# Row softmax with a relative-position bias: the bias table issued first, three one-row chunks at the head of the stream, one bias strip buffer in place of two

## The chip, the cores and the metric

The kernel runs on one core of one Trainium2 chip. The metric is the device time in microseconds (us) of the whole program. The engines are named as in the profile: DVE is VectorE, ACT is ScalarE, POOL is GpSimd, SP is the sync engine that only issues transfers here. TensorE is not used.

## The reference, cut to what matters

```python
B, H, S, max_rel = 2, 8, 2112, 16
rel = pos[:, None] - pos[None, :]
bias = rel_bias[:, np.clip(rel, -16, 16) + 16]       # (H, S, S), from a table of (H, 33)
x = logits + bias[None]
out = softmax(x, axis=-1)                             # float32, (B, H, S, S)
```

The logits are 285 MB and so is the result. There are about three passes of arithmetic over each element, so the kernel is a stream: load, add, exponential, multiply, store.

## The kernel before: the parts that the change and the argument touch

The 2112 rows of one head are cut in 64 blocks of 33 rows. Two heads (one "head pair" k) fill the 128 partitions, and a chunk is r rows of every block: normally r = 3, which is 3.24 MB and 25 KB per partition. One bias strip F for a head pair, 128 x 2144, serves all chunks of that pair, read at a shifted offset.

```python
fpool = ctx.enter_context(tc.tile_pool(name="fpool", bufs=2))    # bias strips
io = ctx.enter_context(tc.tile_pool(name="io", bufs=7))          # chunks of up to 3 rows
# ... (chunks: r = 3 everywhere, the very last three rows one by one)

NPRE = 2
pre = [load(c, nc.sync) for c in chunks[:NPRE]]                  # SP queue
rbB = const.tile([P, H // 2, 2, W], FP32, tag="rbB")
nc.scalar.dma_start(out=rbB, in_=...)                            # bias table, ACT's queue
# ... (masks; bias_rows(k) builds F with two passes of 128x2112 and small ones)

for n, c in enumerate(chunks):
    k, row, j, r = c
    if k != fk:
        F, fk = bias_rows(k), k
    L = pre[n] if n < NPRE else load(c, nc.gpsimd)               # POOL's queue
    nc.vector.tensor_tensor(out=L3, in0=L3, in1=F3, op=ALU.add)
    for i in range(r):
        nc.scalar.activation(out=x, in_=x, func=EXP, accum_out=tot[:, i : i + 1])
    nc.vector.reciprocal(out=tot[:, 0:r], in_=tot[:, 0:r])
    for i in range(r):
        nc.vector.tensor_scalar_mul(out=x, in0=x, scalar1=tot[:, i : i + 1])   # "normalisation"
    nc.sync.dma_start(out=rows(out, row, j, r), in_=L[:, 0 : r * S])           # SP queue
```

A scheduler decides the order of instructions on each engine, and puts in the waits. A buffer of `io` is loaded again ("reload") only when its store has landed.

The softmax here doesn't subtract the row's maximum and nothing guards it: scores larger than these inputs give would overflow.

## Time and profile before

| | before |
|---|---|
| time, median (range) | 1334.06 us (1333.89 to 1334.34, 6 runs) |
| span of the profile | 1332.3 us |
| bytes moved | 571.19 MB |
| rate from 120 to 1260 us | 433 GB/s |

First the page of the kernel before: the span, the engines' busy time, then for 40 equal slices of the span the busy share of the DMA engines in tenths and the rate.

```profile
span 1332.3 us, 1666 instructions
...
DVE 947.2 (71%) x473; ACT 524.9 (39%) x529; POOL 49.0 (4%) x94
...
DMA  9999999999999999999999999999999999999998
GB/s 392 415 402 432 432 435 431 434 431 434 431 434 430 434 431 433 432 432 434 432 434 430 434 432 433 432 434 431 433 434 432 432 432 434 431 432 432 433 428 372
```

DMA is busy in every slice, while DVE has 29% of the span to spare. The bytes at 432.5 GB/s (the steady rate, between 432 and 433) need 571.19 MB / 0.4325 MB per us = 1320.7 us. Only the difference, 11.6 us of the span, can be won by ordering at this rate. I use this "loss" throughout: the length of a stretch minus the bytes it moved divided by 0.4325.

The same kernel cut in windows. Columns: the window, its length, busy us (and number of instructions) of DVE, ACT and POOL, clock, DMA share, GB/s. A packet counts in the window where it starts, so the DMA share can exceed 1.

```profile
core 0: us, DVE busy (x) ACT busy (x) POOL busy (x), PEclk, DMA share, GB/s
0.00:12.00 12.00, 0.00 (x0) 0.00 (x0) 3.31 (x11) 1.00 0.86 319
12.00:54.00 42.00, 36.02 (x21) 19.79 (x20) 0.00 (x0) 1.00 1.01 433
54.00:58.00 4.00, 4.00 (x4) 4.00 (x5) 0.00 (x0) 1.00 0.71 304
58.00:66.00 8.00, 8.00 (x6) 1.28 (x2) 0.00 (x0) 1.00 0.96 409
66.00:69.00 3.00, 3.00 (x3) 1.50 (x1) 0.53 (x1) 1.00 0.96 406
69.00:77.00 8.00, 8.00 (x7) 4.45 (x6) 0.00 (x0) 1.00 1.05 348
...
120.00:1260.00 1140.00, 812.33 (x395) 452.00 (x456) 41.49 (x76) 1.00 1.00 433
```

Before 120 us the loss sits mainly in the first 12 us, at 54 to 58 us and at 66 to 77 us (another 4.8 us are lost after 120 us). The loads and stores that make it, from the timeline of the kernel before (start, duration, engine, line, operation, output<-input, count; a queue such as SPq is where a transfer is issued, and a count over 1 means that the duration covers several with gaps):

```profile
0.73 0.40 ACTq L71 DMA_DIRECT2D rbB<-in_rel_bias_dram  x1
0.74 0.86 SPq L64 DMA_DIRECT2D L<-in_logits_dram  x2
...
24.15 2.35 DVE L120 TENSOR_TENSOR F<-eq,rbP 128x2112 f32<-128x2112 f32 x1
26.42 20.08 DVE L140 TENSOR_TENSOR L<-L,F 128x6336 f32<-128x6336 f32 x3
...
53.22 7.46 DVE L148 TENSOR_SCALAR L<-L,tot 128x2112 f32<-128x2112 f32 x6
...
57.02 4.03 SPq L149 DMA_DIRECT2D out_dram<-L  x2
...
66.54 0.53 POOL L64 DMA_DIRECT2D L<-in_logits_dram  x1 [62.40 <-DMA out_dram<-L]
```

All seven buffers are filled by 56 us. The first store is issued at 57.02, the first reload at 66.54, when that store has landed. The first packet of that reload appears only at 72.48, 5.9 us after its issue. Note the line at 24.15: the second strip's first pass, which DVE runs ahead of the first add.

### The profile page before, as it was taken

The numbers are of one execution on the slowest core, as the hardware profiler recorded it, in microseconds if no ns is written. First come the engines' busy times: TensorE is split into PE (matmuls) and PEld (weight loads), VectorE is DVE, ScalarE is ACT, GpSimd is POOL, SyncE is SP. The second block draws the span as 40 slices with busy tenths as digits, with TensorE's granted clock in tenths as the row PEclk, the third lists the DMA queues.
The fourth block names the chain that finished last, engine by engine and source line by source line (L and its number), as shares of the span: only waits on it lengthen the run. The fifth ranks groups of instructions, "written<-read, shape, count | busy, mean of one in ns | idle before, by whom it ended". The sixth has DMA issues, their size and how long they took to land.

```text
span 1332.3 us, 1666 instructions
## 1 busy us (share of the span) xinstructions
DVE 947.2 (71%) x473; ACT 524.9 (39%) x529; POOL 49.0 (4%) x94
## 2 busy tenths in 40 slices
DVE  4997677669676677767966677766796677766773
ACT  0754334433344333443344333443334333443341
POOL 0000000000000000000000000000000000000000
DMA  9999999999999999999999999999999999999998
GB/s 392 415 402 432 432 435 431 434 431 434 431 434 430 434 431 433 432 432 434 432 434 430 434 432 433 432 434 431 433 434 432 432 432 434 431 432 432 433 428 372
DMA packets 26076, 571.19 MB, mean 429 GB/s; under 512 B 2896, under 2 KB 3024, under 8 KB 3024
## 3 DMA queue, kind: packets, MB, share of 16 engines
q1 hardware_dynamic: 13248, 291.97, 51.0%
q0 software_dynamic: 12672, 278.99, 48.8%
q10 hardware_dynamic: 144, 0.14, 0.0%
q14 instruction: 12, 0.10, 0.0%
HBM read 285.61 MB, written 285.47 MB: 429 GB/s over the span
## 4 chain that ended last, share of the span: by engine, by line
DMA 79%; DVE 11%; issue 7%; another core or an unknown queue 1%; ACT 0%; POOLq 0%; POOL 0%; ACTq 0%
DMA out_dram<-L 47%; DMA L<-in_logits_dram 30%; DVE L L148 6%; DVE L L140 4%; DMA rbB<-in_rel_bias_dram 1%; DVE F L121 0%; DVE F L120 0%; ACT L L144 0%; DVE tot L145 0%; POOLq L64 0%; POOL L L64 0%; DVE rest L100 0%; DVE rest L101 0%; DVE rbP L92 0%
## 5 line engine op out<-in xcount | busy, mean ns | idle before, releaser
L140 DVE TENSOR_TENSOR L<-L,F 128x6336 f32<-128x6336 f32 (+1 forms) x90 | 594.7, 6609 | 346.8 <-DMA L<-in_logits_dram 346.6
L144 ACT ACTIVATE L<-L 128x2112 f32<-128x2112 f32 x264 | 515.2, 1952 | 768.7 <-DVE L L140 756.5
L148 DVE TENSOR_SCALAR L<-L,tot 128x2112 f32<-128x2112 f32 x264 | 331.8, 1313 | 0.0
L64 POOL DMA_DIRECT2D L<-in_logits_dram x88 | 48.5, 551 | 1241.2 <-DMA out_dram<-L 1231.6
L144 ACT ACTIVATION_READ_ACCUMULATOR L<-L 128x1 f32 x264 | 49.2, 186 | 0.0
L145 DVE RECIPROCAL tot<-tot 128x3 f32<-128x3 f32 (+1 forms) x90 | 14.8, 167 | 0.9 <-ACT L L144 0.9
L91 DVE COPY rbP<-rbB 64x132 f32<-64x132 f32 x1 | 0.2, 223 | 17.9 <-DMA rbB<-in_rel_bias_dram 17.9
L121 DVE TENSOR_TENSOR F<-F,rest 128x2112 f32<-128x2112 f32 x4 | 9.4, 2344 | 0.0
L120 DVE TENSOR_TENSOR F<-eq,rbP 128x2112 f32<-128x2112 f32 x4 | 9.4, 2344 | 0.0
L144 ACT ACT_TABLE_LOAD x1 | 1.3, 1283 | 17.8 <-DMA L<-in_logits_dram 17.8
L101 DVE SCALAR_TENSOR_TENSOR rest<-gt,rbP,rest 128x64 f32<-128x64 f32 x4 | 1.0, 265 | 0.0
L100 DVE TENSOR_SCALAR rest<-lt,rbP 128x64 f32<-128x64 f32 x4 | 0.9, 240 | 0.0
L122 DVE COPY F<-rbP 128x16 f32<-128x16 f32 x4 | 0.7, 163 | 0.0
L123 DVE COPY F<-rbP 128x16 f32<-128x16 f32 x4 | 0.7, 167 | 0.0
L78 POOL IOTA qm<- 64x64 f32 x2 | 0.4, 176 | 0.4 <-PEq L175 0.4
L92 DVE COPY rbP<-rbB 64x132 f32<-64x132 f32 x1 | 0.2, 225 | 0.0
L89 DVE TENSOR_SCALAR lt<-qm 128x64 f32<-128x64 f32 x1 | 0.2, 186 | 0.0
L89 DVE TENSOR_SCALAR gt<-qm 128x64 f32<-128x64 f32 x1 | 0.2, 186 | 0.0
L89 DVE TENSOR_SCALAR eq<-qm 128x64 f32<-128x64 f32 x1 | 0.2, 185 | 0.0
L164 POOL MEMSET const-float32-0.0<- 128x1 f32 x1 | 0.1, 98 | 0.2 <-issue 0.2
L164 POOL MEMSET const-bfloat16-1.0<- 128x1 bf16 x1 | 0.1, 101 | 0.0
L164 POOL MEMSET const-float32-1.0<- 128x1 f32 x1 | 0.1, 98 | 0.0
(1 smaller groups left out, 0.1 us busy)
## 6 DMA issues: line engine op xcount, KB each, us to landing
out_dram<-L SPq DMA_DIRECT2D x87, 3168.0 KB, 38.2
L<-in_logits_dram POOLq DMA_DIRECT2D x85, 3168.0 KB, 25.7
L<-in_logits_dram SPq DMA_DIRECT2D x2, 3168.0 KB, 24.3
L<-in_logits_dram POOLq DMA_DIRECT2D x3, 1056.0 KB, 17.0
out_dram<-L SPq DMA_DIRECT2D x3, 1056.0 KB, 18.3
rbB<-in_rel_bias_dram ACTq DMA_DIRECT2D x1, 132.0 KB, 17.2
```

Source lines behind the costliest of these rows:

```text
L64: eng.dma_start(out=L[:, 0 : r * S], in_=rows(logits, row, j, r))
L89: nc.vector.tensor_scalar(out=m, in0=qm, scalar1=0.0, scalar2=None, op0=op)
L100: nc.vector.tensor_scalar(out=rest, in0=lt, scalar1=low, scalar2=None, op0=ALU.mult)
L101: nc.vector.scalar_tensor_tensor(out=rest, in0=gt, scalar=high, in1=rest, op0=ALU.mult, op1=ALU.add)
L120: nc.vector.tensor_tensor(out=blocks, in0=wide(eq), in1=rev, op=ALU.mult)
L121: nc.vector.tensor_tensor(out=blocks, in0=blocks, in1=wide(rest), op=ALU.add)
L122: nc.vector.tensor_copy(out=F[:, 0:MR], in_=low.to_broadcast([P, MR]))
L123: nc.vector.tensor_copy(out=F[:, FW - MR : FW], in_=high.to_broadcast([P, MR]))
L140: nc.vector.tensor_tensor(out=L3, in0=L3, in1=F3, op=ALU.add)
L144: nc.scalar.activation(out=x, in_=x, func=EXP, accum_out=tot[:, i : i + 1])
L145: nc.vector.reciprocal(out=tot[:, 0:r], in_=tot[:, 0:r])
L148: nc.vector.tensor_scalar_mul(out=x, in0=x, scalar1=tot[:, i : i + 1])
```

## The change

The intent is to have the pipeline start earlier: the table arrives first, the first three chunks are a third as long so that compute and stores begin sooner, and one strip buffer keeps the second strip's work from standing ahead of the first add.

```diff
--- before.py
+++ after.py
@@ -34,16 +34,17 @@
     FW = S + W - 1
 
     const = ctx.enter_context(tc.tile_pool(name="const", bufs=1))
-    fpool = ctx.enter_context(tc.tile_pool(name="fpool", bufs=2))
+    fpool = ctx.enter_context(tc.tile_pool(name="fpool", bufs=1))
     io = ctx.enter_context(tc.tile_pool(name="io", bufs=7))
     small = ctx.enter_context(tc.tile_pool(name="small", bufs=8))
 
     chunks = []
     for k in range(H // 2):
         for b in range(B):
-            last = k == H // 2 - 1 and b == B - 1
             sizes = [R] * (W // R)
-            if last:
+            if not chunks:
+                sizes = [1] * R + sizes[1:]
+            if k == H // 2 - 1 and b == B - 1:
                 sizes = sizes[:-1] + [1] * R
             j = 0
             for r in sizes:
@@ -64,14 +65,14 @@
         eng.dma_start(out=L[:, 0 : r * S], in_=rows(logits, row, j, r))
         return L
 
-    NPRE = 2
-    pre = [load(c, nc.sync) for c in chunks[:NPRE]]
-
     rbB = const.tile([P, H // 2, 2, W], FP32, tag="rbB")
     nc.scalar.dma_start(
         out=rbB,
         in_=bass.AP(tensor=rel_bias.tensor, offset=rel_bias.offset, ap=[[0, P], [1, H * W]]),
     )
+    NPRE = 4
+    pre = [load(c, nc.sync) for c in chunks[:NPRE]]
+
 
     qm = const.tile([P, NB], FP32, tag="qm")
     for p0 in (0, NB):
```

The number of chunks goes from 90 to 92. The prefill (what is loaded before any buffer is stored) goes from 7 x 3.24 = 22.7 MB to 3 x 1.08 + 4 x 3.24 = 16.2 MB, because a one-row chunk still takes a whole buffer.

## The prediction

> **What bounds it now.** DMA. The page gives 571.19 MB over a 1332.3 us span; its slices show DMA at nine tenths or more in 38 of 40, VectorE (DVE) 71% busy, ScalarE 39%. The transfer view cut into windows gives 433 GB/s from 92 to 1260 us, so at that rate the bytes alone need about 1320 us. The Trainium skill, "DMA: Bandwidth & Descriptors", section "Where 436 GB/s comes from", has a ceiling of 435 GB/s; the trace agrees within 1%. Only some 12 us are lost: about 6.7 (2.9 MB missing) before 92 us, about 5 after 1310 us.
>
> **The loss at the start (transfer view, windows).** 2 to 12 us runs at 329 to 359 GB/s; 54 to 58 us at 304, because all loads end at 56 and the first store leaves at 57.0; 72 to 77 us at 314, because the first reload is issued only at 66.5, when the first store has landed, and its packets appear at 72.2. The two holes miss 1.1 MB, 2.5 us.
>
> **What the change does.**
> 1. The bias table moves ahead in the program, but it was already first on ScalarE's queue (issued 0.73 us, loads 0.74). The order buys nothing. It took 17.2 us because its small packets alternate with 25 KB packets of two load queues (skill, same page, "Queues, rings and completion order": round robin between queues at packet granularity; the trace agrees: table and first load land together near 17.8). Beside 8.4 KB packets I estimate 6 to 9 us.
> 2. The second strip's first multiply (2.35 us) no longer sits ahead of the first add: strip ready 6.3 us after the table, first add at about 14 us instead of 26.4.
> 3. Three one-row chunks: first store issued at about 27 us, not 57. But VectorE's order puts two normalisations after the third add, the third after the fourth chunk's add. The stores also queue behind the fourth chunk's 3.2 MB load, so they move at about 38 us. The prefill falls from 22.7 to 16.2 MB, loads end near 41 us, and the first reload can be issued only near 42 and moves near 47: one hole of about 2 us near 45 in place of the two.
> 4. One strip buffer: at the three head changes the strip (two operations of 2.35 us) is built between the last add of one head pair and the first of the next. VectorE idles 4.5 us per 15 us chunk, stores take 38 us from issue to landing, and before already delayed that add by 5 us with transfers at 432. I expect nothing.
>
> On the critical path is only what refills DMA holes: estimate 1 to 4 us. Compute starting 12 us earlier is not 12 us saved.
>
> **Prediction.** 1332.3 us, range 1328.5 to 1335.5. Faster by over 2%: 0.01; within 2%: 0.98; slower by over 2%: 0.01.
>
> **What would show it.** Right: bytes unchanged; 432 to 433 GB/s in mid-run, head changes included (near 315, 645, 975 us); first add at 11 to 17 us; first store issued before 32 us; table landing in 6 to 10 us; the holes at 56 and 73 gone, one near 45; mean over the first 92 us up from 401 to 405-415 GB/s; tail unchanged. Step 4 is wrong if a head change drops below 425 GB/s; step 3 if more or larger holes appear.
>
> **What would make it wrong.** A longer stall of the reloads behind three small stores; a steady-state split between load and store queues in which a head change starves both; small packets less efficient than estimated; the tail shifting since chunk numbering moves by two.

## The result, and the profile after

| | before | after |
|---|---|---|
| time, median (range) | 1334.06 us (1333.89 to 1334.34, 6 runs) | 1339.94 us (1336.88 to 1340.91, 6 runs) |
| span of the profile | 1332.3 us | 1334.4 us (an execution of 1336.92 us) |
| loss of the profiled span until 120 us | 6.8 us | 8.8 us |
| loss of the profiled span after 120 us | 4.8 us | 4.9 us |

Ratios are the mean time of one kernel's fast runs over that of the other's of the same rounds, so not quite the ratio of the medians that are quoted. Here it is 1.0038, interval 1.0025 to 1.0051. The kernel became 0.4% slower, not 0.1% faster, and its times scatter over 4 us where those of before lie within half a us. The profile is of one of its faster executions.

The page of the kernel after, span, DMA busy tenths and rate:

```profile
span 1334.4 us, 1678 instructions
...
DMA  9999999999999999999999999999999999999998
GB/s 388 394 406 431 432 434 432 433 432 432 433 432 433 433 432 432 430 434 432 432 435 429 435 433 431 435 428 436 431 432 433 430 435 432 432 434 430 435 428 375
```

The second slice (33 to 67 us) is lower than before (394 for 415), the third a little higher (406 for 402), and from the fourth on the two differ by a few GB/s either way. The windows of the kernel after, with the columns of the table before:

```profile
0.00:12.00 12.00, 3.50 (x10) 1.28 (x1) 2.28 (x9) 1.00 0.87 309
12.00:54.00 42.00, 24.23 (x17) 10.77 (x11) 1.06 (x2) 1.00 1.00 418
54.00:58.00 4.00, 4.00 (x3) 2.05 (x3) 0.00 (x0) 1.00 0.90 374
58.00:66.00 8.00, 8.00 (x3) 7.22 (x9) 0.00 (x0) 1.00 0.97 417
66.00:69.00 3.00, 3.00 (x4) 3.00 (x4) 0.53 (x1) 1.00 0.63 135
69.00:77.00 8.00, 8.00 (x4) 3.51 (x5) 0.00 (x0) 1.00 1.01 393
...
120.00:1260.00 1140.00, 814.64 (x394) 451.93 (x457) 40.09 (x76) 1.00 1.00 432
```

The holes of before at 54 to 58 us and at 69 to 77 us have shrunk: 374 for 304 GB/s and 393 for 348. In their place is a deeper one at 66 to 69 us, 135 GB/s, and the stretch from 12 to 54 us runs at 418 instead of 433. In loss: 0 to 54 us 3.1 us before and 4.8 after; 54 to 78 us 3.5 and 3.6; 78 to 120 us 0.2 and 0.3. So between 54 and 78 us nothing was won, and the extra loss of this execution, 2.0 us, lies nearly all before 54 us. From 120 us on nothing differs in these two profiles. (This is one of the faster executions; the one under "again" lost more on both sides of 120 us.)

The timeline of the kernel after, the lines that answer to those of before:

```profile
14.79 2.36 DVE L141 TENSOR_TENSOR L<-L,F 128x2112 f32<-128x2112 f32 x1
...
32.33 1.83 SPq L150 DMA_DIRECT2D out_dram<-L  x2
...
42.61 6.76 DVE L141 TENSOR_TENSOR L<-L,F 128x6336 f32<-128x6336 f32 x1 [8.75 <-DMA L<-in_logits_dram]
...
49.29 1.31 DVE L149 TENSOR_SCALAR L<-L,tot 128x2112 f32<-128x2112 f32 x1
...
50.63 0.33 SPq L150 DMA_DIRECT2D out_dram<-L  x1
...
66.13 0.53 POOL L65 DMA_DIRECT2D L<-in_logits_dram  x1 [17.39 <-DMA out_dram<-L]
...
67.75 0.33 SPq L150 DMA_DIRECT2D out_dram<-L  x1
```

The compute does start 12 us earlier (first add at 14.79 for 26.42), and the first stores leave at 32.33 for 57.02. But the third small store leaves only at 50.63, because its normalisation (49.29) stands behind the add of the fourth chunk (42.61), which waits for that chunk's load. The last packets of this store are seen between 65 and 66 us, and only then is the buffer's reload issued, 66.13. The next store follows at 67.75. At that moment all earlier loads are through, and the queues are dry.

Part of why a 1.08 MB store takes 15 us shows in the transfer view of the kernel after from 57 to 63 us (queue, packets, MB, share of 16 engines; q0 is POOL's queue, here loads with 25 KB packets, q1 is SP's, here that store with 8.4 KB packets):

```profile
DMA packets 154, 2.49 MB, mean 415 GB/s; under 512 B 3, under 2 KB 3, under 8 KB 3
...
q0 software_dynamic: 75, 1.82, 70.5%
q1 hardware_dynamic: 79, 0.67, 26.3%
```

The two queues send about as many packets, 75 and 79, so the store gets 0.67 of 2.49 MB. The first of its packets appear at 54 us, 3.4 us after the issue; why so late is not shown.

### The profile page after: what moved, and what is told of

Read it like the earlier page. It is cut to its first block, busy times and chain, and to the rows that moved or that the text cites. A ratio compares the mean times of both kernels' runs of the same rounds, so it can differ in the third digit from the quotient of the medians.

```text
span 1334.4 us, 1678 instructions
## 1 busy us (share of the span) xinstructions
DVE 947.8 (71%) x477; ACT 525.1 (39%) x529; POOL 48.2 (4%) x94
## 4 chain that ended last, share of the span: by engine, by line
DMA 79%; DVE 10%; issue 8%; another core or an unknown queue 1%; ACT 0%; SPq 0%; POOLq 0%; POOL 0%; ACTq 0%
DMA out_dram<-L 44%; DMA L<-in_logits_dram 35%; DVE L L149 6%; DVE L L141 3%; DVE F L121 0%; ACT L L145 0%; SPq L65 0%; DVE tot L146 0%; POOLq L65 0%; POOL L L65 0%; ACTq L176 0%; ACTq L145 0%; POOLq L176 0%
```

## The experiments

All but the last three were timed in 5 rounds against the kernel before on the same chip. Theory A: the loss is in when the early stores land, above all the third small one, and so when their buffers can be reloaded. Rivals: the single strip stalls the head changes (B); the lead chunks shift the tail (C); small first packets beside the table lose the time in the first 6 us (D).

| run | median us (range) | ratio to before (interval) | loss to 120 us | loss after |
|---|---|---|---|---|
| again (the change, once more) | 1339.66 (1338.69 to 1341.29) | 1.0041 (1.0028 to 1.0053) | 10.5 | 7.6 |
| no_leads | 1330.71 (1330.65 to 1331.11) | 0.9974 (0.9960 to 0.9988) | 3.4 | 4.8 |
| two_strips | 1352.31 (1352.12 to 1352.54, 4 runs) | 1.0135 (1.0121 to 1.0149) | 19.4 | 10.1 |
| fourth_on_pool | 1332.39 (1332.24 to 1332.98) | 0.9986 (0.9974 to 0.9999) | 4.4 | 5.1 |
| one_strip | 1331.09 (1330.72 to 1331.15) | 0.9976 (0.9964 to 0.9989) | 3.5 | 5.0 |
| third_on_act | 1332.97 (1332.76 to 1333.16) | 0.9991 (0.9978 to 1.0003) | 4.9 | 5.2 |
| lead_in_one | 1331.17 (1331.01 to 1331.40) | 0.9977 (0.9964 to 0.9991) | 3.6 | 4.6 |
| slow_mul | 1339.84 (1339.54 to 1340.14) | 1.0042 (1.0030 to 1.0055) | 10.9 | 6.1 |
| table_on_sync | 1331.45 (1330.93 to 1331.53) | 0.9979 (0.9965 to 0.9992) | 4.1 | 4.8 |

The two losses are those of the profiled execution. The kernel before had medians of 1334.2 to 1334.4 us in these jobs.

### again: the change, unchanged

No edit.

> The changed kernel unchanged, to get more executions and a second profile. Its six timed runs fell in two groups, 1336.9 (two) and 1339.7 to 1340.9 (four), and the profile is of the lower one. Theory A (the reload of a buffer waits for small stores that crawl beside large load packets, and the queues run dry near 67 us): the two groups again, and if the profile falls in the upper group, the extra 3 us lie before 100 us as a longer or further hole in the transfers, with 432 to 433 GB/s after it. Rival B (one strip buffer stalls the three head changes): the extra lies near 315, 645 or 975 us. Rival C (the lead chunks shift the tail): the extra lies after 1290 us.

1338.69 to 1341.29 us in five runs: not the two groups that were expected, and none near 1336.9. The profile is of the slowest, 1341.29. Between 120 and 1260 us it stays at 432 GB/s, head changes included, so rival B has no support. It lost 1.7 us more than the first profile before 120 us, as Theory A said, but also 2.7 us more after it, 2.4 of them after 1260 us, which Theory A did not say. Neither theory alone explains the scatter; the looks at the end of this section return to it.

The part before 120 us shows in the timeline of this execution: the reload at 66.15 took 1.62 us to issue instead of 0.53, inside the three normalisations that DVE ran from 63.89.

```profile
63.89 3.77 DVE L149 TENSOR_SCALAR L<-L,tot 128x2112 f32<-128x2112 f32 x3
...
66.15 1.62 POOL L65 DMA_DIRECT2D L<-in_logits_dram  x1 [17.41 <-DMA out_dram<-L]
...
67.68 0.33 SPq L150 DMA_DIRECT2D out_dram<-L  x1
```

From 66 to 72 us this execution moved 0.96 MB and the first profile 1.60 MB.

### no_leads: the change without the one-row chunks

```diff
-            if not chunks:
-                sizes = [1] * R + sizes[1:]
...
-    NPRE = 4
+    NPRE = 2
```

> Table first and one strip buffer, but no one-row chunks and two loads ahead as in the kernel before. Theory A: not slower than before; with one strip the scheduler places the first normalisation after the third add instead of the fourth, so the first store leaves near 48 us instead of 57, the hole at 56 us goes and the one at 73 shrinks: 1332 to 1333.5 us, all runs in one group. Rival B (one strip buffer costs): 1336 us or more, with rates under 425 GB/s at a head change. Table lands near 17 us as before.

1330.71 us, all runs within 0.5 us: faster than Theory A asked for, and 3.6 us faster than before. The first store leaves at 49.95 us. Its windows have no hole left:

```profile
54.00:66.00 12.00, 12.00 (x6) 5.95 (x6) 0.41 (x1) 1.00 1.01 433
66.00:78.00 12.00, 12.00 (x7) 6.43 (x7) 0.65 (x2) 1.00 1.00 431
```

So what is left of the change when the lead chunks are taken out is a gain, and rival B falls: with one strip buffer the head changes run at the same rate.

### two_strips: the change with two strip buffers

```diff
-    fpool = ctx.enter_context(tc.tile_pool(name="fpool", bufs=1))
+    fpool = ctx.enter_context(tc.tile_pool(name="fpool", bufs=2))
```

> The changed kernel with two strip buffers again. The built order puts the first normalisation after the fourth chunk's add here. Theory A: slower than the changed kernel, because the first store leaves only near 50 us while all loads are through near 42: a hole of 6 to 8 us from 42 us on, 1340 to 1346 us. Rival B (the single strip is what costs): 1332 to 1335 us.

1352.31 us, slower than expected: 12.7 us above the change beside which it ran. The strip buffer that I had called neutral is worth more than anything else here. Its timeline shows the reason: the first normalisation comes after the fourth chunk's add, and the first store behind it.

```profile
42.49 6.76 DVE L141 TENSOR_TENSOR L<-L,F 128x6336 f32<-128x6336 f32 x1 [11.68 <-DMA L<-in_logits_dram]
49.17 1.31 DVE L149 TENSOR_SCALAR L<-L,tot 128x2112 f32<-128x2112 f32 x1
...
50.51 9.58 SPq L150 DMA_DIRECT2D out_dram<-L  x3
```

All loads were through by 42 us, and nothing could be stored. The windows from 36 to 66 us:

```profile
36.00:54.00 18.00, 11.51 (x5) 4.72 (x5) 0.00 (x0) 1.00 0.45 190
54.00:66.00 12.00, 12.00 (x5) 7.18 (x8) 0.53 (x1) 1.00 0.81 296
```

### fourth_on_pool: the fourth chunk loaded by POOL's queue

```diff
-    NPRE = 4
+    NPRE = 3
```

> The changed kernel with the fourth chunk's load issued from GpSimd's queue, so the three one-row stores do not stand behind it, and VectorE's order does not wait for it before the third normalisation. Theory A: small stores leave near 39 to 42 us and land before 51; reloads run from about 48 us; no hole near 67: 1332.5 to 1334.5 us, in one group. Rival D (small first packets beside the table lose the time in the first 6 us): still 1336 us or more.

1332.39 us, just under the expected range, 7.3 us below the change, in one group. The prefill is 16.2 MB here too, so a small prefill is not what costs. The loss of the first 12 us is the same as in the change (309 GB/s there, 313 here), so rival D has no part in the difference. The edit does two things at once. The fourth load no longer stands ahead of the small stores on SP's queue. And the order is another: all three small normalisations now stand behind the fourth chunk's add, but that add runs at 30.54 us, because its data come early by the other queue, so the first store is issued at 38.54 and the third at 41.28 (the change: 32.33 and 50.63). Standing behind the fourth add is thus harmless when that add need not wait. The next but one experiment frees the third normalisation alone.

### one_strip: the kernel before with one strip buffer

```diff
-    fpool = ctx.enter_context(tc.tile_pool(name="fpool", bufs=2))
+    fpool = ctx.enter_context(tc.tile_pool(name="fpool", bufs=1))
```

> The kernel before with one strip buffer and nothing else. Its built VectorE order is that of the kernel without lead chunks, which ran at 1330.7 us. If the single strip, by letting the scheduler place the first normalisation after the third add, is the whole gain there, this too runs at 1330.3 to 1331.2 us and the table's place in the program is worth nothing. If the table's place helped, 1332 to 1334 us.

1331.09 us, as the kernel without lead chunks (0.9976 and 0.9974 of before). So the place of the table in the program is worth nothing measurable, and the single strip is the whole gain of that kernel. In the built order of before, the second strip's first pass and four adds stand ahead of the first normalisation; with one buffer that pass must wait, and the scheduler places the first normalisation after the third add. The first store leaves at 49.9 us instead of 57.0.

### third_on_act: only the third small chunk's normalisation moved to ScalarE

```diff
+            if n == 2:
+                nc.scalar.mul(x, x, tot[:, i : i + 1])
+            else:
                 nc.vector.tensor_scalar_mul(out=x, in0=x, scalar1=tot[:, i : i + 1])
```

> The changed kernel, only the normalisation of the third one-row chunk done on ScalarE, so its store need not wait for the fourth chunk's add. Theory A1 (the hole near 67 us is the third small store, issued at 50.6 us behind the fourth chunk's add and then crawling beside 25 KB load packets until 65.7, so that the reload of its buffer is issued only at 66.1): third store issued near 36 us, landed by 51, reload issued by 53, no hole at 66 to 72 us; 1333.5 to 1335.5 us and all runs within 1 us. Rival A2 (any prefill of 16 MB instead of 23 runs dry there whatever the third store does): hole at 66 to 69 us stays, 1336.5 to 1341 us.

1332.97 us, within 0.4 us in all runs, a little better than expected. The third store is issued by 36.3 us and the reloads at 45.65, 48.15 and 51.39 us, where the change had 45.7, 48.2 and 66.1:

```profile
32.26 3.98 SPq L153 DMA_DIRECT2D out_dram<-L  x3
...
45.65 0.53 POOL L65 DMA_DIRECT2D L<-in_logits_dram  x1 [42.54 <-DMA out_dram<-L]
48.15 0.53 POOL L65 DMA_DIRECT2D L<-in_logits_dram  x1 [1.98 <-DMA out_dram<-L]
51.39 0.53 POOL L65 DMA_DIRECT2D L<-in_logits_dram  x1 [2.71 <-DMA out_dram<-L]
```

One 2 us operation out of 264, on another engine, takes away 6.7 us of the median (against again, on another chip) and the scatter. This is Theory A1, and A2 falls.

### lead_in_one: a repair that keeps the lead chunks

The three one-row chunks share one full buffer, and NPRE is 3.

```diff
+        i = len(got)
+        if 0 < i < R:
+            L = got[0][:, i * S :]
+        else:
+            L = io.tile([P, R * S], FP32, tag="L", name="L")
+        got.append(L)
```

> A repair: the three one-row chunks share one full-size buffer, and all other early loads go to GpSimd's queue, so the prefill stays 22.7 MB. Theory A: loads last to about 56 us, first stores leave near 39 us, no hole over 0.5 us before 100 us; cumulative loss at 120 us about 4 us (3.5 of it in the first 6 us, as in the changed kernel): 1331 to 1332.5 us, no better than the kernel with one strip alone, since the lead chunks cost about 0.3 us at the start and there is no hole left for them to fill.

1331.17 us, as expected: no better than one strip alone. With the holes gone there is nothing for an earlier start to fill.

### slow_mul: the early normalisations in another form

```diff
+            if 3 <= n < 9:
+                nc.vector.tensor_tensor(out=x, in0=x,
+                    in1=tot[:, i : i + 1].to_broadcast([P, S]), op=ALU.mult)
+            else:
                 nc.vector.tensor_scalar_mul(out=x, in0=x, scalar1=tot[:, i : i + 1])
```

> The changed kernel, with the normalisation of chunks 3 to 8 written as a multiply of two tensors, which I estimate at 2.3 us a row, as the add of one row takes, instead of 1.31. Theory E (the spread of 1336.9 to 1341.3 us comes from GpSimd's reload issue falling into a normalisation on VectorE, which makes it last 0.8 to 1.6 us instead of 0.53 and delays its packets while the queues are empty): no reload issue before 105 us longer than 0.6 us, and the five runs within 0.8 us; the stores leave 3 us or more later, so the mean itself is no better, 1338 to 1342 us. Rival (the spread comes from elsewhere): runs spread over 2 us or more as before.

The five runs lie within 0.6 us, at 1339.84, and in the profile every reload before 105 us was issued in 0.53 us: both as Theory E asked. The median is no better than that of the change, as expected, and five runs are few to call a scatter gone. The short issues came though the normalisations (now about 2.3 us a row) ran at the same moment:

```profile
63.87 6.89 DVE L150 TENSOR_TENSOR L<-L,tot 128x2112 f32<-128x2112 f32 x3
...
66.07 0.53 POOL L65 DMA_DIRECT2D L<-in_logits_dram  x1 [17.39 <-DMA out_dram<-L]
86.05 0.53 POOL L65 DMA_DIRECT2D L<-in_logits_dram  x1 [19.45 <-issue]
97.56 0.53 POOL L65 DMA_DIRECT2D L<-in_logits_dram  x1 [10.98 <-DMA out_dram<-L]
```

The Trainium skill, "SBUF — State Buffer", section "Who interferes with whom", says that a `tensor_scalar` of VectorE can hold a port pair that it shares with GpSimd, and that a transfer issued by GpSimd then waits because its descriptors cannot be written, while `tensor_tensor` has no such mode; with both inputs in SBUF, as here, it shares only the read side with GpSimd, which the page infers does not stop the writing of descriptors. The runs agree in this: inside the `tensor_scalar` normalisations the issue took 1.62 us in one profile, inside the `tensor_tensor` form 0.53. It is not longer each time: in the first profile after, the issue at 66.13 us also fell into a normalisation and took 0.53. Nor does a short issue make an early start: here the reload issued at 86.05 us moved its first packet only at 91.76. Whether Theory E is the whole of the scatter is another question.

### table_on_sync: the table truly first

no_leads, with one more edit; the table's line stands ahead of the loads there.

```diff
-    nc.scalar.dma_start(
+    nc.sync.dma_start(
         out=rbB,
```

> The kernel without lead chunks and with one strip (1330.7 us), the table now truly first: on the SP queue, ahead of the loads, instead of on a queue of its own. The table should land near 5 us instead of 17.7, because its packets alternate with nothing until GpSimd's loads start near 5 us; the first add then waits for the first load, at 15 to 18 us instead of 24. If holes alone decide, this gains nothing, since that kernel has no hole left after 12 us; what can change is the loss of the first 12 us (3.1 us there), by 1 us either way: 1329.7 to 1331.5 us. If an earlier start of the compute were worth its own length, 6 us, it would be 1325 us.

1331.45 us, at the upper edge of the range. The table landed 4.9 us after its issue and the first add began at 18.95 us instead of 24.2, and nothing was gained: 5 us of earlier compute are worth nothing when no hole is left. In this profile the 88 reload and load issues of POOL average 0.94 us, against 0.55 in the kernel before, and the run is none the slower for it: a long issue by itself cost nothing here.

### look2, look3, look4: three more profiles of the change

No edit, single runs of unknown state. 

> The changed kernel, one more profile, to see what separates its executions near 1337 us from those near 1340. The two profiles so far lost 8.8 and 10.5 us before 120 us, and 4.9 and 7.6 us after it, the latter with the 16 increments of a late store spread over 4.2 and 6.7 us. If Theory E is the whole of it, an execution whose GpSimd issue at 66 us lasts 0.53 us is near 1337 and one where it lasts over 0.8 us is near 1340. If the spread of the 16 engines at the end decides instead, the time follows that spread whatever the issue at 66 us took.

> As the look before it: a further profile of the same kernel. Theory E: time and the length of the GpSimd issue at 66 us go together. Rival: time and the spread of the 16 engines at the end go together, whatever that issue took.

> As the look before it: a further profile of the same kernel. Theory E: time and the length of the GpSimd issue at 66 us go together. Rival: time and the spread of the 16 engines at the end go together, whatever that issue took.

In the traces the semaphore of each transfer is incremented 16 times; I read this as once for each of the 16 DMA engines. The last column is the time from the first to the last of the 16 for one store, the median of the stores that landed after 1300 us. It is read from the packed traces, which record these increments, and no view of `prof` prints it.

| profile | time us | issue at 66 us | loss to 120 us | loss after | 16 increments apart |
|---|---|---|---|---|---|
| before | 1334.24 | (none) | 6.8 | 4.8 | 3.9 |
| after | 1336.92 | 0.53 | 8.8 | 4.9 | 4.0 |
| again | 1341.29 | 1.62 | 10.5 | 7.6 | 6.1 |
| look2 | 1338.24 | 0.53 | 8.6 | 6.4 | 5.4 |
| look3 | 1336.37 | 0.69 | 8.6 | 4.8 | 3.6 |
| look4 | 1352.94 | 0.69 | 8.7 | 21.2 | 9.8 |

Theory E is not the whole of it. Between look3 and look2, 1.9 us apart, the loss until 120 us is equal and the slower one has the shorter issue (0.53 us for 0.69); what differs is how far apart the 16 increments of the last stores came. The span cannot end before the last of them. Both terms add: of the 4.4 us between the first two profiles of the change, 1.7 us were lost before 120 us and 2.7 us after, while the increments moved 2.2 us further apart. look4 is 0.9% above the slowest other run of this kernel: in it the increments were at most 5.6 us apart until 700 us and up to 23 us after 1250 us. I set it aside as an outlier; its cause is not known. What sets the increments apart stays open. The other profiles fit: in the seven kernels without the hole at 66 us or a larger one (before among them) they are 3.9 to 4.5 us apart at the end and the loss after 120 us is 4.6 to 5.2 us; slow_mul has 4.8 and 6.1 us, two_strips, with the largest hole, 8.5 and 10.1. So the extra loss at the end was seen only in kernels with such a hole, but how the one would lead to the other is not shown. Three of the seven keep the one-row chunks, so these alone do not shift the tail, and rival C falls.

## Why the prediction was wrong, point by point

- **The bound was right.** 432 to 433 GB/s from 120 to 1260 us in both kernels, bytes unchanged, and the start of compute 12 us earlier was indeed not 12 us saved.
- **Step 1, the table.** Right: its place in the program is worth nothing (one_strip and no_leads agree within 0.4 us), and beside small packets it lands earlier, 7.7 us after its issue, inside 6 to 10.
- **Step 2, the first add.** Right: 14.79 us for an expected 14.
- **The signs asked for.** Besides the holes, two failed: the first small store was issued at 32.33 us, not near 27, because it stands behind the third add (28.49); and the mean rate over the first 92 us fell from 401 to 393 GB/s instead of rising to 405 to 415.
- **Step 3, "one hole of about 2 us near 45 in place of the two". This is the step that failed.** The hole near 45 came, with 0.9 us lost from 45 to 51. A second one, from 66 us on, was not foreseen; 54 to 78 us lost 3.6 us, as much as the two old holes in that stretch. The prediction treated the three small stores as one group that moves at about 38 us. It had written down that the third normalisation stands behind the fourth chunk's add, but did not follow it to the reload: fourth load landed 42.6, add until 49.3, store issued 50.6, its last packets after 65, reload issued 66.1. It also left out that a queue's share goes by packets, which it had used for the table: 8.4 KB packets beside 25 KB ones get about a quarter of the bytes. third_on_act moves that one normalisation, and the loss in that stretch falls from 3.6 to 0.6 us, in all to 4.9 us before 120 us. This step does not account for all of the slowdown. The first profiled execution is 2.7 us above that of before: 2.0 before 120 us, 0.1 after, 0.6 outside the span. The one under again is 7.0 us above: 3.7, 2.8 and 0.6. The 2.8 us at the end are gone in third_on_act too, but have no shown mechanism; the 0.6 us are the time minus the span, 2.5 us for the change and 1.9 for before, and stay open as well.
- **Step 4, one strip buffer: "I expect nothing".** Right at the head changes, wrong in all. The single strip changes the scheduler's order in the first 60 us: 3.1 us gained on its own (one_strip), 12.7 us inside the change (two_strips against again). The two parts of the change therefore pull apart: the strip gains, the lead chunks with their load on SP's queue lose more.
- **The tail.** Unchanged in the profile taken first (4.8 and 4.9 us), but 7.6 and 6.4 us in two others. The range allowed for no scatter because before had none.

The versions that beat both kernels by most are one_strip and no_leads (1331.09 and 1330.71 us, 0.9976 and 0.9974 of before); lead_in_one and table_on_sync (0.9977 and 0.9979) do more and gain no more. What the first two leave is 3.4 to 3.5 us at the start and 4.8 to 5.0 us at the end.

## What to carry to other kernels

In a stream that the transfers bound, an earlier start of compute is worth only the dry stretches of the queues that it fills; find those first, as windows below the steady rate, and follow each early buffer from its store's issue to its reload. A small transfer need not be a quick one when it shares the engines with large packets (here 1.08 MB took 15 us), and one small instruction that stands behind a wait in an engine's order can hold a buffer back for 15 us. When a buffer count changes, compare the built order of instructions around the start and not only the place where the buffer is reused.

## What the Trainium skill lacked or had wrong

- "DMA: Bandwidth & Descriptors", section "Queues, rings and completion order", describes round robin between queues by packets. It does not say what follows for sizes: from 57 to 63 us the store with 8.4 KB packets got 0.67 of 2.49 MB beside loads with 25 KB packets, and the 1.08 MB took 15 us to land.
- The same page, section "Where 436 GB/s comes from", says that the memory side, about 358 GB/s, binds transfers between HBM and SBUF. This core, the only one that the program uses, moved 432 to 433 GB/s for 1140 us, half reads and half writes. The page has the condition elsewhere (a note under its measured bandwidths gives about 358 GB/s to each core when both cores of a memory domain stream); the passage lacks it.
- The same page gives about 1 us to the first byte of a transfer issued by GpSimd. One reload here began to move 1.2 us after its issue (45.72, first packet at 46.96), but the first load of the kernel before, issued at 1.38 us, showed its first packet only at 5.38, with VectorE idle, and that kernel's first reload, issued at 66.54, at 72.48. What makes the difference is not shown.
- "SBUF — State Buffer", section "Who interferes with whom", agrees with the runs (1.62 against 0.53 us), but does not say that the block can miss: in another execution the issue inside the same normalisation took 0.53 us.
- "DMA: Bandwidth & Descriptors" has, in "Latency and other measured facts", two engines that are usually slower. No page that I found has what such a spread costs: here the 16 increments of one store come 3.6 to 6.1 us apart at the end of an ordinary execution of the changed kernel, and the executions with more of it lost more at the end (4.8 to 7.6 us after 120 us).
